# One decoder step in fp32 by split matmuls: which weight pieces are split ahead of time, and where the halves are kept

## The chip, the cores and the metric

The kernel runs on one core of a Trainium2 chip. The metric is the device time of one execution in microseconds (us); the time before is the median of three runs.

## The reference

A prompt of 256 tokens and 32 sample tokens (8 sequences of 4) go through two layers of width 2048. Each layer has a mixer and a dense squared-ReLU network, with an RMS norm ahead of and behind each. Cut to what the change touches:

```python
def _odd_mixer(h, conv_hist, w_in, ..., w_out):
    z = h @ w_in                                   # 2048 x 4096
    u, v, a, gate = jnp.split(z, [...])
    u = jax.nn.gelu(u)
    v = _ln(jax.nn.gelu(v), sg_ln_g, sg_ln_b)
    mixed = jnp.einsum('gij,bnjgc->bnigc', ws, vc) + sg_b   # causal gating within a chunk
    yc = u * mixed
    glu = a * jax.nn.sigmoid(gate)
    conv = depthwise_conv(concat([conv_hist, glu]), dw_w) + dw_b   # 31 taps, 1024 channels
    yd = jax.nn.silu(_ln(conv, cv_ln_g, cv_ln_b))
    return concat([yc, yd]) @ w_out

for l in range(2):                                 # l = 0: the even mixer (pooling, retention)
    h = h + _rms(mixer(_rms(h, ...)), ...)
    f = _rms(h, ...)
    f = jnp.square(jax.nn.relu(f @ w_up[l])) @ w_down[l]    # 2048 -> 8192 -> 2048
    h = h + _rms(f, ...)
```

## The kernel before

All 288 tokens stand as columns, features as partitions. A product of fp32 values is made of three fp32r matmuls: weights and activations are each split into a rounded part (`hi`) and the rest (`lo`), and hi·hi, lo·hi and hi·lo are summed in PSUM.

**Subs.** The weights come in 720 pieces, called subs, of 256 rows by 512 columns (512 KB). A sub is 24 matmuls (line 604): 2 row blocks, 4 column blocks `m`, 3 products. Eight subs (four in the odd layer's output projection) make a group, which fills four PSUM banks; the banks are read out behind its last sub (evictions). The subs in order: 0 to 79 input of the even mixer, 80 to 111 its output, 112 to 367 the first dense network (groups `w_up` and `w_down`, in four quarters), 368 to 431 input of the odd mixer, 432 to 463 its output in two halves, 464 to 719 the second dense network.

**How a sub is fed.** SP issues the load of `raw` (four buffers). ACT rounds it into `whi`, DVE subtracts into `wlo`: `A.activation(out=hi, in_=raws[p], func=AF.Copy)` in `emit_hi` and `V.tensor_tensor(out=lo, in0=raws.pop(p), in1=f(hi), op=SUB)` in `emit_lo`. `whi` and `wlo` have a ring of 3 slots, plus 1 (odd mixer) or 2 (dense networks) from a pool that is opened and closed by stage. A slot is free when TensorE has used its sub.

**Jobs and kept subs.** 60 subs of the odd mixer and of the second dense network's first group are split ahead. For each a job stands in the first dense network, behind its subs 1 and 5 of a group (`JOBS`): its raw load, ACT and DVE work are as a sub's, it takes a slot of the ring, and both halves are written to DRAM (`hik`, `lok`). Where the sub is due, SP loads both halves into its slot, with no work of ACT or DVE.

**Order of the work.** Each engine takes its instructions in the order in which `run` writes them. Around each sub, `run` writes the feeding of later subs, the sub's matmuls, evictions behind a last sub, and a step of each background generator (a `yield` ends a step). The odd mixer's background work is the convolution (`conv_all` on DVE with sums in PSUM, tile `cacc`; `conv_slow` on ACT and GpSimd; a load meter holds both back), the gating with its layer norm (`gating`), and behind the convolution `conv_out`: `layer_norm`, then Silu and splitting of 8 tiles. What is left of `conv_out` behind sub 447 is written at once (`bg_drain`), since sub 448 reads it.

**Norm boundaries.** The last group's squares are summed by one-column matmuls (`sum_part`), the last of them behind the last sub; then the scale is computed, spread and applied. `keep_warm` issues matmuls whose result nobody reads.

Of the kernel before, what the change touches and what calls it, by code (L numbers as in the profile page):

```python
# [178 lines left out]
def build(tc, ctx, I, O, C):  # L179
# [231 lines left out]
    def last_tiles(src, m):  # L411
# [61 lines left out]
    feed, pos, nraw, parts, kept = [], [], [], {}, {}  # L473
    RAW, RING = 4, 3
    JOBS = (1, 5)
# [16 lines left out]
    def emit_dma(p):  # L492
        kind, i = feed[p]
        if kind == "kept":
            return
# [16 lines left out]
    def emit_hi(p):  # L512
        kind, i = feed[p]
        hi, lo = parts[p] = ring_slot()
        if kind == "kept":
            for a, b in zip((hi, lo), kept[i]):
                SP.dma_start(out=f(a), in_=b)
        else:
            A.activation(out=hi, in_=raws[p], func=AF.Copy)
        if kind != "job":  # L520
            his[i] = hi, lo

    def emit_lo(p):
        kind, i = feed[p]
        hi, lo = parts.pop(p)
        if kind != "kept":
            V.tensor_tensor(out=lo, in0=raws.pop(p), in1=f(hi), op=SUB)
# [8 lines left out]
    def plan():  # L536

        todo = []
        where = {}
        at = 0  # L540
        for gi, g in enumerate(groups):
            for s in range(g.nsub):
                subs.append((g, s))
                if g.ahead and g.ahead(s):
                    todo.append(at + s)
            where[gi] = at
# [4 lines left out]
        ahead = set(todo)  # L551
        for i in range(len(subs)):
            pos.append(len(feed))
            feed.append(("kept" if i in ahead else "sub", i))
            if i in slots:
                feed.append(("job", slots[i]))
        n = 0
        for kind, i in feed:
            nraw.append(n)
            n += kind != "kept"  # L560
        nraw.append(n)

    def fetch():
        while W["dma"] < len(feed) and nraw[W["dma"]] < nraw[W["split"]] + RAW:
            emit_dma(W["dma"])
            W["dma"] += 1
# [14 lines left out]
    def some(n):  # L581

        return min(W["split"] + n - 1, pos[W["now"]] + RING + W["extra"] - 1)
# [66 lines left out]
    def run():  # L650
# [3 lines left out]
        for i, (g, s) in enumerate(subs):  # L654
# [29 lines left out]
            if last:  # L684
                if g.defer:
# [5 lines left out]
                    def rest(g=g):  # L691
                        yield from finish_pre(g.ready)
                        for m in range(0 if g.keep else 4):
# [36 lines left out]
    def ffn(layer, last):  # L730
        wu, wd = ("w_up", layer), ("w_down", layer)
        for q in range(4):
            for gm in range(4):
# [11 lines left out]
                def st_up(q=q, gm=gm):  # L745
                    if gm == 0:
# [4 lines left out]
                                  start=st_up, kouter=first, defer=first, jobs=() if last or first else JOBS,  # L751
                                  ahead=(lambda s: True) if last and first else None))
            for gm in range(4):
                def ev_dn(m, ps, gm=gm, q=q):
# [5 lines left out]
                    if q == 3:  # L760
# [3 lines left out]
                        else:  # L764
                            last_tiles(y(k), m)

                def fin_dn(q=q, gm=gm):
                    if q == 3 and gm == 3:
                        for m in range(4):
# [7 lines left out]
                                  jobs=() if last or (q == 3 and gm == 3) else JOBS))  # L777
# [331 lines left out]
    def even():  # L1109
# [35 lines left out]
        for gm in range(4):  # L1145
            def ev_o(m, ps, gm=gm):
# [5 lines left out]
                else:  # L1152
                    last_tiles(ps, m)
# [188 lines left out]
    def layer_norm(src, n, total, by_pe=False):  # L1342

        yield
        yield
# [25 lines left out]
        yield  # L1371
# [105 lines left out]
    def conv_out():  # L1477
# [4 lines left out]
        for k in range(8):  # L1482
# [6 lines left out]
            if k % 2 == 1:  # L1489
                yield  # L1490

    def odd():
# [9 lines left out]
        def ga(j):  # L1502
            def post_ga():
                if j == 1:
                    bg_drain(st_["setup"])
                if j == 0:
                    while "begun" not in Q:
# [9 lines left out]
                              ahead=lambda s: j == 0 or s % 2 == 1))  # L1517

        def vgrp(gm):
            def post_v():  # L1520
                if gm == 1:
# [5 lines left out]
                              post=post_v, ahead=lambda s: s % 2 == 1))  # L1527

        def ugrp(gm):
            def post_u():  # L1530
                if gm == 1:
                    bg_drain(st_["gate"])

                    def tail():
                        while any(c in bgs or c in fills for c in st_["conv"]):
# [7 lines left out]
                              start=start_u if gm == 0 else None, post=post_u, ahead=lambda s: s % 2 == 1))  # L1543
# [3 lines left out]
        for half in range(2):  # L1547
            for gm in range(4):
                def ev_o(m, ps, gm=gm, half=half):
# [5 lines left out]
                    else:  # L1555
# [4 lines left out]
                        else:  # L1560
                            last_tiles(y(k), m)

                def post_o(gm=gm, half=half):
                    if half == 0 and gm == 3:
                        for c in st_["conv"]:
# [13 lines left out]
                                  ahead=lambda s: s % 2 == 1))  # L1579
# [130 lines left out]
```

## Time and profile before

| | |
|---|---|
| runs | 2469.9, 2473.21, 2479.39 us; median 2473.21 |
| profiled execution | 2476.82 us, of it the span 2475.1 us |
| busy share of the span | TensorE 98%, DVE 55%, ACT 44%, GpSimd 10% |
| granted TensorE clock, mean | 0.988 |
| DMA | 529.35 MB, mean 214 GB/s |

How to read it: the span is the time from the first to the last instruction. TensorE's busy share counts pipelined matmuls and says little; what a stage loses is seen by its length against the number of its subs. Idle time of another engine costs something only where TensorE waits for it.

### The profile page before, as it was taken

To read this page: it belongs to the slowest core of one execution; us is meant where nothing else is said; L and a number is where in the kernel's file an instruction comes from. 1 tells how busy PE (TensorE), PEld (TensorE's weight loads), DVE (VectorE), ACT (ScalarE), POOL (GpSimd) and SP (SyncE) were. 2 spreads that over 40 slices of the span, in tenths; PEclk is the share of its full clock that TensorE was granted. 3 is DMA by queue.
4 is the path that set the end of the run, shared out by engine and by line. 5 is a ranking of instruction groups with operands and counts; after the bars stand their busy time and mean duration, and the time that the engine had idled before them with its cause. 6 is when DMAs were issued, how large, how long until landed. Compare 5 with 4: busy or idle time off the path is not lost.

```text
span 2475.1 us, 43388 instructions
## 1 busy us (share of the span) xinstructions
PE 2420.7 (98%) x17976; PEld 2386.2 (96%) x17976; DVE 1360.7 (55%) x1844; ACT 1090.6 (44%) x1567; POOL 251.9 (10%) x293
## 2 busy tenths in 40 slices
PE   9999999999999999999999999899999999999997
PEld 8899999999999999999999999899999999999997
DVE  5665564764455556555546976346434544544453
ACT  5343443554544455455434443435434434433442
POOL 0521111000000000000114750100000000000011
PEclk9999999999999999999999999999999999999998
DMA  7555464588888888888775656455555554545552
GB/s 253 164 185 181 159 206 160 181 280 296 289 289 297 279 295 290 294 288 293 261 254 211 246 200 219 179 196 190 168 164 168 163 169 161 172 162 170 165 166 92
DMA packets 146871, 529.35 MB, mean 214 GB/s; under 512 B 16809, under 2 KB 17849, under 8 KB 146649
## 3 DMA queue, kind: packets, MB, share of 16 engines
q1 hardware_dynamic: 142240, 511.81, 60.4%
q0 software_dynamic: 4288, 14.71, 1.8%
q8 instruction: 140, 2.29, 0.4%
q14 instruction: 59, 0.48, 0.1%
q10 hardware_dynamic: 144, 0.07, 0.0%
HBM read 453.68 MB, written 73.87 MB: 213 GB/s over the span
## 4 chain that ended last, share of the span: by engine, by line
PE 84%; DVE 6%; DMA 4%; ACT 3%; issue 2%; SPq 0%; POOL 0%; DVEq 0%; ACTq 0%; POOLq 0%
PE mm L604 81%; DVE wlo L162 2%; DVE cacc L162 2%; DMA raw<-in_wt 2%; DMA wlo<-lok 1%; ACT whi L162 1%; ACT tmp L162 1%; PE ms L313 1%; DMA lok<-wlo 1%; PE po L995 1%; DVE tmp L162 1%; PE ms L999 0%; DVE conv L162 0%; DVE yo L162 0%; PE ms L303 0%
## 5 line engine op out<-in xcount | busy, mean ns | idle before, releaser
L162 DVE TENSOR_TENSOR wlo<-raw,whi 128x1024 fp32r<-128x1024 f32 (+1 forms) x721 | 886.9, 1240 | 751.1 <-ACT whi L162 737.3
L162 ACT ACTIVATE whi<-raw 128x1024 fp32r<-128x1024 f32 (+1 forms) x721 | 755.1, 1057 | 1011.2 <-PE mm L604 892.1
L604 PE MATMUL mm<-xhi,wlo 128*128 128x288 f32 x3200 | 944.9, 297 | 11.3 <-DVE wlo L162 9.2
L604 PE MATMUL mm<-xhi,whi 128*128 128x288 f32 x3200 | 944.2, 297 | 10.3 <-DVE tmp L162 6.2
L604 PE MATMUL mm<-xlo,whi 128*128 128x288 f32 x3200 | 919.6, 296 | 0.0
L604 PE MATMUL mm<-hidhi,whi 128*128 128x288 f32 x2560 | 754.8, 296 | 6.8 <-ACT whi L162 3.2
L604 PE MATMUL mm<-hidhi,wlo 128*128 128x288 f32 x2560 | 757.6, 297 | 2.5 <-DMA wlo<-lok 1.7
L604 PE MATMUL mm<-hidlo,whi 128*128 128x288 f32 x2560 | 745.2, 296 | 0.0
L604 PEld LDWEIGHTS mm<-xhi,wlo 128*128 128x128 f32 x3200 | 605.4, 189 | 16.0 <-DVE wlo L162 13.2
L604 PEld LDWEIGHTS mm<-xhi,whi 128*128 128x128 f32 x3200 | 605.9, 189 | 13.3 <-issue 6.8
L604 PEld LDWEIGHTS mm<-xlo,whi 128*128 128x128 f32 x3200 | 595.8, 189 | 0.5 <-DVE xlo L162 0.5
L604 PEld LDWEIGHTS mm<-hidhi,whi 128*128 128x128 f32 x2560 | 485.3, 190 | 8.1 <-ACT whi L162 3.4
L604 PEld LDWEIGHTS mm<-hidhi,wlo 128*128 128x128 f32 x2560 | 485.4, 190 | 3.3 <-DMA wlo<-lok 2.1
L604 PEld LDWEIGHTS mm<-hidlo,whi 128*128 128x128 f32 x2560 | 480.3, 189 | 0.0
L162 POOL TENSOR_TENSOR acc<-acc,tmp 128x288 f32<-128x288 f32 x55 | 53.3, 970 | 1657.1 <-ACT tmp L162 1654.3
L162 DVE TENSOR_TENSOR y<-mm,y 128x288 f32<-128x288 f32 x112 | 50.9, 457 | 103.3 <-PE mm L604 103.3
L162 DVE SCALAR_TENSOR_TENSOR u<-mm,rb 128x288 f32<-128x288 f32 x120 | 54.3, 457 | 71.2 <-PE mm L604 71.2
L162 DVE SCALAR_TENSOR_TENSOR cacc<-gx,vecs,cacc 128x256 f32<-128x256 f32 x168 | 68.5, 478 | 0.0
L162 ACT ACTIVATE hidhi<-u 128x288 fp32r<-128x288 f32 x128 | 56.9, 445 | 4.1
L162 ACT ACTIVATE u<-u 128x288 f32<-128x288 f32 x128 | 55.3, 432 | 7.0 <-DVE u L162 6.9
L162 POOL TENSOR_TENSOR conv<-conv,tap 128x256 f32<-128x256 f32 x60 | 53.7, 895 | 13.6 <-ACT tap L162 10.0
L162 DVE TENSOR_TENSOR hidlo<-u,hidhi 128x288 fp32r<-128x288 f32 x128 | 49.7, 450 | 0.0
(180 smaller groups left out, 909.8 us busy)
## 6 DMA issues: line engine op xcount, KB each, us to landing
raw<-in_wt SPq DMA_DIRECT2D x719, 512.0 KB, 4.2
hik<-whi SPq DMA_DIRECT2D x60, 512.0 KB, 6.4
lok<-wlo SPq DMA_DIRECT2D x60, 512.0 KB, 7.1
whi<-hik SPq DMA_DIRECT2D x60, 512.0 KB, 4.4
wlo<-lok SPq DMA_DIRECT2D x60, 512.0 KB, 5.8
s0t<-in_state_ret POOLq DMA_DIRECT2D x24, 256.0 KB, 3.3
out<-s0t POOLq DMA_DIRECT2D x24, 256.0 KB, 3.4
out<-yo SPq DMA_DIRECT2D x8, 288.0 KB, 2.4
```

What stands on the lines that cost most here:

```text
L162: return call(*args, **kw)
L313: PE.matmul(P["sums"][:, t:t + 1], lhsT=a[:, c:c + 128], rhs=ones[:, 0:1], start=first and t == 0, stop=last and t == 2)
L604: PE.matmul(ps, lhsT=lhsT[:, k, c], rhs=rhs, start=s == 0 and k == 0 and which == 0, stop=s == g.nsub - 1 and k == 1 and which == 2)
L995: PE.matmul(po[gq:gq + 32, 0:256], lhsT=E["qdm"][:, hh, 32 * (b + i):32 * (b + i + 1)], rhs=s[:, i, :], start=False, stop=b >= 4, tile_pos ...
```

## The change

- **What is kept.** Only the `lo` half is written to DRAM and loaded back (`kept`); `hi` of such a sub is made again from `raw` where the sub is due, so its weights are loaded once more. DVE has nothing to do for it.
- **Where jobs put their halves.** Into buffers of their own (`jhi` once, `jlo` three times), no longer into slots of the ring.
- **Which subs.** All 64 of the odd mixer's input, and the 8 of the second dense network's first group. Those of the odd mixer's output are named too (every second sub of half 0, 8 in all), but the lambda reads `half` when `plan` runs, behind the loop, where it is 1: none of them is kept. So 72 jobs are made, not 80.
- **Where the jobs stand.** Behind subs 3, 5 and 7 of a group, from the third `w_up` group on.
- **Steps.** In `layer_norm` for the convolution two `yield`s go, and `conv_out` ends a step after four tiles, not two. `flush` (pending `hidlo` work) is called ahead of a deferred group's evictions.
- **A matmul.** `last_sums` issues `keep_warm(1)` ahead of the last sum, at three of the four boundaries.

```diff
-    JOBS = (1, 5)
+    JOBS = (3, 5, 7)
...
     def emit_hi(p):
         kind, i = feed[p]
-        hi, lo = parts[p] = ring_slot()
-        if kind == "kept":
-            for a, b in zip((hi, lo), kept[i]):
-                SP.dma_start(out=f(a), in_=b)
-        else:
-            A.activation(out=hi, in_=raws[p], func=AF.Copy)
-        if kind != "job":
-            his[i] = hi, lo
+        if kind == "job":
+            parts[p] = [W["pool"].tile([128, 2, 512], F32R, tag=t, name=t, bufs=n) for t, n in (("jhi", 1), ("jlo", 3))]
+            A.activation(out=parts[p][0], in_=raws[p], func=AF.Copy)
+            return
+        hi, lo = parts[p] = his[i] = ring_slot()
+        A.activation(out=hi, in_=raws[p], func=AF.Copy)
+        if kind == "lo":
+            SP.dma_start(out=f(lo), in_=kept[i])
...
         if kind == "job":
-            kept[i] = [dram.tile([128, 2, 512], F32, tag=f"{t}{i}", name=f"{t}k") for t in ("hi", "lo")]
-            W["out"] = [(b, a) for a, b in zip((hi, lo), kept[i])]
+            kept[i] = dram.tile([128, 2, 512], F32, tag=f"k{i}", name="kept")
+            W["out"] = [(kept[i], lo)]
...
-        return min(W["split"] + n - 1, pos[W["now"]] + RING + W["extra"] - 1)
+        return min(W["split"] + n - 1, pos[min(W["now"] + RING + W["extra"], len(subs)) - 1])
...
-                                  start=st_up, kouter=first, defer=first, jobs=() if last or first else JOBS,
-                                  ahead=(lambda s: True) if last and first else None))
+                                  start=st_up, kouter=first, defer=first, jobs=() if last or (q == 0 and gm < 2) else JOBS,
+                                  ahead=(lambda s: "lo") if last and first else None))
...
         elif i == 1:
             sum_part(P.pop(("own", 2)))
+            if P.pop("rest"):
+                keep_warm(1)
             sum_part(P.pop(("own", 3)), last=True)
...
     def layer_norm(src, n, total, by_pe=False):
 
         yield
-        yield
+        if not by_pe:
+            yield
...
-                              ahead=lambda s: j == 0 or s % 2 == 1))
+                              ahead=lambda s: "lo"))
...
-                                  ahead=lambda s: s % 2 == 1))
+                                  ahead=lambda s: "lo" if half == 0 and s % 2 else None))
```

Three places show how instructions move. First DVE in the odd mixer's input, up to the eviction (`tmp<-mm,rb`) behind sub 399; `cacc` and `conv` are the convolution. Before:

```order
L162 SCALAR_TENSOR_TENSOR cacc<-gx,vecs,cacc 128x256 x4
L162 TENSOR_TENSOR wlo<-raw,whi 128x1024
L162 TENSOR_REDUCE conv<-prod 128x32
L162 TENSOR_SCALAR conv<-conv,vecs 128x32
L162 SCALAR_TENSOR_TENSOR cacc<-gx,vecs,cacc 128x256 x8
L162 TENSOR_TENSOR wlo<-raw,whi 128x1024
L162 SCALAR_TENSOR_TENSOR cacc<-gx,vecs,cacc 128x256 x15
L162 TENSOR_TENSOR tmp<-mm,rb 128x288 x4
```

And in the changed kernel, up to the same eviction:

```order
L162 TENSOR_REDUCE conv<-prod 128x32
L162 TENSOR_SCALAR conv<-conv,vecs 128x32
L162 SCALAR_TENSOR_TENSOR cacc<-gx,vecs,cacc 128x256 x6
L162 SCALAR_TENSOR_TENSOR conv<-gx,vecs,cacc 128x256
L162 SCALAR_TENSOR_TENSOR cacc<-gx,vecs,cacc 128x256
L162 TENSOR_TENSOR conv<-cacc,conv 128x256
L162 TENSOR_SCALAR cacc<-gx,vecs 128x256 x2
L162 SCALAR_TENSOR_TENSOR cacc<-gx,vecs,cacc 128x256 x18
L162 TENSOR_TENSOR tmp<-mm,rb 128x288 x4
```

The `wlo` rows are gone, and convolution work stands in their place. Second, DVE at the convolution's layer norm (`conv<-conv,mean`) and behind it (`tmp<-conv,rl`, `hidlo`). Before, where sub 448's `wlo` is the last one ahead of `tmp<-conv,rl`, and three more pairs of the last two rows follow with no `wlo` between them:

```order
L162 TENSOR_TENSOR conv<-cacc,conv 128x256
L162 TENSOR_TENSOR wlo<-raw,whi 128x1024 x2
L162 TENSOR_TENSOR conv<-conv,mean 128x288 x8
L162 TENSOR_TENSOR wlo<-raw,whi 128x1024
L162 TENSOR_SCALAR sm_86<-ms 128x3
L162 TENSOR_TENSOR wlo<-raw,whi 128x1024
L162 TENSOR_TENSOR tmp<-conv,rl 128x288 x2
L162 TENSOR_TENSOR hidlo_16946<-tmp,hidhi_16945 128x288 x2
```

In the changed kernel, beginning at the eviction behind sub 431; the four `wlo` in one row are those of subs 437 to 440:

```order
L162 TENSOR_TENSOR tmp<-mm,rb 128x288 x4
L162 TENSOR_TENSOR wlo<-raw,whi 128x1024
L162 TENSOR_TENSOR tmp<-mb,ug 128x288 x4
L162 TENSOR_TENSOR hidlo_16332<-tmp,hidhi_16331 128x288 x4
L162 TENSOR_TENSOR conv<-conv,mean 128x288 x4
L162 TENSOR_TENSOR wlo<-raw,whi 128x1024
L162 TENSOR_TENSOR conv<-conv,mean 128x288 x4
L162 TENSOR_TENSOR wlo<-raw,whi 128x1024
L162 TENSOR_SCALAR sm_86<-ms 128x3
L162 TENSOR_TENSOR wlo<-raw,whi 128x1024 x4
L162 TENSOR_TENSOR tmp<-conv,rl 128x288 x4
```

The layer norm stands eight subs earlier, and the tiles behind it are done near sub 441, not behind sub 447. On TensorE its one-column sums move from ahead of subs 442 and 443 to ahead of subs 434 and 435. Third, SP in the odd mixer's input, with what each issue waits for (`DMAHW` is an earlier transfer). Before:

```order
L503 DMA raw<-in_wt 128x1024 [waits DMAHW3_49,DVE_49]
L517 DMA whi<-hik 128x1024 [waits DMAHW5_49,DMAHW4_49,PE_49]
L517 DMA wlo<-lok 128x1024 [waits DMAHW6_49]
L503 DMA raw<-in_wt 128x1024 [waits DVE_49]
L517 DMA whi<-hik 128x1024 [waits DMAHW7_49,DMAHW1_49,PE_49]
```

And in the changed kernel:

```order
L522 DMA wlo<-kept 128x1024 [waits DMAHW7_49,PE_49]
L504 DMA raw<-in_wt 128x1024 [waits DMAHW0_49,Activation_49]
L522 DMA wlo<-kept 128x1024 [waits DMAHW1_49,PE_49]
L504 DMA raw<-in_wt 128x1024 [waits DMAHW2_49,Activation_49]
L522 DMA wlo<-kept 128x1024 [waits DMAHW3_49,PE_49]
```

A raw load here waits for ACT, no longer for DVE, and two loads a sub follow each other through all 64 subs.

## Rows read from the trace of the kernel before

**Rows 1.** Windows, weight matmuls (line 604) alone: busy us of PE, PEld; PEclk; DMA.

```profile
405.20:437.10 31.90, 25.78 (x194) 25.33 (x192) 1.00 0.42 133
437.10:548.80 111.70, 106.44 (x769) 103.70 (x770) 0.98 0.68 233
548.80:1234.20 685.40, 685.40 (x5186) 685.40 (x5186) 1.00 0.84 289
1234.20:1268.30 34.10, 26.06 (x195) 25.41 (x193) 0.95 0.70 230
1268.30:1327.20 58.90, 54.23 (x385) 52.83 (x386) 0.97 0.69 257
1327.20:1505.60 178.40, 159.84 (x1153) 156.91 (x1153) 0.97 0.60 215
1505.60:1569.90 64.30, 57.30 (x385) 55.84 (x385) 0.92 0.53 189
1569.90:1592.60 22.70, 16.91 (x97) 16.02 (x97) 0.85 0.52 193
1592.60:1640.10 47.50, 38.51 (x291) 38.09 (x289) 0.93 0.71 262
1640.10:1744.30 104.20, 102.62 (x769) 101.91 (x770) 1.00 0.50 167
```

**Rows 2.** Waits of PE from 1327.2 to 1505.7 us: sum, times, longest.

```profile
PE mm L604 <- DVE tmp L162: 8.3, 4, 3.0
PE ms L1439 <- DVE mb L162: 2.9, 1, 2.9
```

**Rows 3.** Waits of PE from 1268.3 to 1327.2 us.

```profile
PE mm L604 <- DMA wlo<-lok: 2.0, 2, 1.2
PE mm L604 <- DMA whi<-hik: 1.3, 1, 1.3
```

**Rows 4.** Waits of PE from 1569.9 to 1592.6 us.

```profile
PE mm L604 <- ACT whi L162: 3.2, 1, 3.2
...
PE mm L604 <- DVE wlo L162: 0.9, 1, 0.9
```

**Rows 5.** Windows, all engines: PE, PEld, DVE, ACT, POOL; PEclk; DMA share, GB/s.

```profile
1327.20:1505.60 178.40, 167.19 (x1233) 165.18 (x1233) 149.79 (x291) 76.21 (x140) 109.84 (x117) 0.97 0.60 215
1356.47:1359.88 3.41, 3.41 (x16) 3.41 (x15) 3.31 (x7) 0.00 (x0) 1.74 (x4) 0.50 0.00 0
```

**Rows 6.** Groups of DVE by form, 1327.2 to 1505.6 us.

```profile
L162 DVE SCALAR_TENSOR_TENSOR cacc<-gx,vecs,cacc 128x256 f32<-128x256 f32 x153 | 62.3, 478 | 0.0
L162 DVE TENSOR_TENSOR wlo<-raw,whi 128x1024 fp32r<-128x1024 f32 x24 | 38.0, 1582 | 13.1 <-ACT whi L162 13.1
```

**Rows 7.** Timeline of DVE ahead of the group end at 1355 us.

```profile
1340.03 1.23 DVE L162 TENSOR_TENSOR wlo<-raw,whi 128x1024 fp32r<-128x1024 f32 x1 [4.20 <-ACT whi L162]
1346.15 3.12 DVE L162 TENSOR_TENSOR wlo<-raw,whi 128x1024 fp32r<-128x1024 f32 x1
1349.19 5.96 DVE L162 SCALAR_TENSOR_TENSOR cacc<-gx,vecs,cacc 128x256 f32<-128x256 f32 x15
```

**Rows 8.** Timeline of POOL at the same place.

```profile
1345.09 3.10 POOL L162 TENSOR_TENSOR prod<-gx,vecs 128x992 f32<-128x992 f32 x1
```

**Rows 9.** Timeline of PE: three unread matmuls at a boundary; wait ahead of the last sum.

```profile
435.34 1.70 PE L369 MATMUL ms<-acc,cg 128*128 128x288 f32 x6
...
1633.27 1.44 PE L313 MATMUL ms<-cg,tmp 128*128 128x1 f32 x6 [0.52 <-ACT tmp L162]
```

**Rows 10.** Windows, all engines, columns as in rows 5: two stretches of dense loads.

```profile
5.00:15.00 10.00, 7.81 (x50) 6.64 (x49) 7.26 (x13) 7.53 (x13) 0.00 (x0) 1.00 1.01 399
1264.00:1296.00 32.00, 30.85 (x211) 29.23 (x210) 20.33 (x43) 10.76 (x23) 3.10 (x5) 0.95 0.86 313
```

**Rows 11.** Page, DMA issues: count, KB each, median us to landing.

```profile
wlo<-lok SPq DMA_DIRECT2D x60, 512.0 KB, 5.8
```

**Rows 12.** Chain of waits: start us, us, what.

```profile
1264.01 12.57 DMA wlo<-lok
```

More of the change, by code (lines that the diff above doesn't have):

```diff
@@ L409, in scale_y, with last_tiles @@
         A.activation(out=y(k), in_=y(k), func=AF.Copy, scale=gain(which, layer, k))
-    def last_tiles(src, m):
+    def last_tiles(src, m, rest):
+        P["rest"] = rest
         if m < OWN:
@@ L472, in build @@
     subs = []
-    feed, pos, nraw, parts, kept = [], [], [], {}, {}
+    feed, pos, parts, kept = [], [], {}, {}
     RAW, RING = 4, 3
-    JOBS = (1, 5)
+    JOBS = (3, 5, 7)
     raws, his = {}, {}
@@ L493, in emit_dma @@
         kind, i = feed[p]
-        if kind == "kept":
-            return
         g, s = subs[i]
@@ L525, in emit_lo @@
         hi, lo = parts.pop(p)
-        if kind != "kept":
-            V.tensor_tensor(out=lo, in0=raws.pop(p), in1=f(hi), op=SUB)
+        raw = raws.pop(p)
+        if kind != "lo":
+            V.tensor_tensor(out=lo, in0=raw, in1=f(hi), op=SUB)
         if kind == "job":
-            kept[i] = [dram.tile([128, 2, 512], F32, tag=f"{t}{i}", name=f"{t}k") for t in ("hi", "lo")]
-            W["out"] = [(b, a) for a, b in zip((hi, lo), kept[i])]
+            kept[i] = dram.tile([128, 2, 512], F32, tag=f"k{i}", name="kept")
+            W["out"] = [(kept[i], lo)]
     def put_out():
@@ L536, in plan @@
     def plan():
-        todo = []
+        todo, kinds = [], {}
         where = {}
@@ L543, in plan @@
                 subs.append((g, s))
-                if g.ahead and g.ahead(s):
+                kind = g.ahead(s) if g.ahead else None
+                if kind:
                     todo.append(at + s)
+                    kinds[at + s] = kind
             where[gi] = at
@@ L550, in plan @@
         slots = dict(zip(slots, todo))
-        ahead = set(todo)
         for i in range(len(subs)):
             pos.append(len(feed))
-            feed.append(("kept" if i in ahead else "sub", i))
+            feed.append((kinds.get(i, "sub"), i))
             if i in slots:
                 feed.append(("job", slots[i]))
[L557 to L561, printed above, removed]
     def fetch():
-        while W["dma"] < len(feed) and nraw[W["dma"]] < nraw[W["split"]] + RAW:
+        while W["dma"] < len(feed) and W["dma"] < W["split"] + RAW:
             emit_dma(W["dma"])
@@ L692, in rest @@
                         yield from finish_pre(g.ready)
+                        flush()
                         for m in range(0 if g.keep else 4):
@@ L764, in ev_dn @@
                         else:
-                            last_tiles(y(k), m)
+                            last_tiles(y(k), m, True)
                 def fin_dn(q=q, gm=gm):
@@ L776, in ffn @@
                                   post=to_odd if q == 3 and gm == 1 and not last else None,
-                                  jobs=() if last or (q == 3 and gm == 3) else JOBS))
+                                  jobs=() if last or (q == 3 and gm > 0) else JOBS))
     evo, ne = _cols(C_EVEN)
@@ L1370, in layer_norm @@
         yield
-        yield
+        if not by_pe:
+            yield
         pb = spread(rs)
@@ L1488, in conv_out @@
             late(lambda hl=hl, s=s, hh=hh: V.tensor_tensor(out=hl, in0=s, in1=f(hh), op=SUB))
-            if k % 2 == 1:
+            if k % 4 == 3:
                 yield
@@ L1526, in vgrp @@
                               lambda m, ps: ev_v_odd(m, ps, gm), start=start_v_odd if gm == 0 else None,
-                              post=post_v, ahead=lambda s: s % 2 == 1))
+                              post=post_v, ahead=lambda s: "lo"))
         def ugrp(gm):
@@ L1542, in ugrp @@
             groups.append(Grp(w, [(512 * gm, 512)], list(range(KT)), xs, lambda m, ps: ev_u(m, ps, gm),
-                              start=start_u if gm == 0 else None, post=post_u, ahead=lambda s: s % 2 == 1))
+                              start=start_u if gm == 0 else None, post=post_u, ahead=lambda s: "lo"))
         for fn, i in ((ga, 0), (ga, 1), (ga, 2), (vgrp, 0), (vgrp, 1), (ga, 3), (ugrp, 0), (ugrp, 1)):
@@ L1560, in ev_o @@
                         else:
-                            last_tiles(y(k), m)
+                            last_tiles(y(k), m, True)
                 def post_o(gm=gm, half=half):
```

3 lines of the change are left out of this document (1 added, 2 removed).

## The prediction

> **What bounds the kernel now.** I read the stages first, by windows that hold the weight matmuls alone [rows 1]. From 548.8 to 1234.2 us, 216 subs take 685.4 us, so a sub that waits for nothing takes 3.173 us; the granted clock there is 1.00. 720 subs at this pace would be 2285 us. What a stage loses is its length less its subs times 3.173:
>
> - 405.2 to 437.1, 8 subs (25.4): 6.5, a norm boundary at full clock
> - 437.1 to 548.8, 32 subs (101.5): 10.2, the start of the first dense network
> - 1234.2 to 1268.3, 8 subs: 8.7, the next boundary
> - 1268.3 to 1327.2, 16 subs (50.8): 8.1, the odd mixer's first two input groups
> - 1327.2 to 1505.6, 48 subs (152.3): 26.1, the rest of its input
> - 1505.6 to 1569.9, 16 subs: 13.5, output half 0, with the convolution's layer norm
> - 1569.9 to 1592.6, 4 subs (12.7): 10.0, the first group of half 1
> - 1592.6 to 1640.1, 12 subs (38.1): 9.4, with a boundary
> - 1640.1 to 1744.3, 32 subs: 2.7, the start of the second dense network
>
> Then the waits of TensorE: in the rest of the odd mixer's input four times the evicting `tmp` of DVE, 8.3 us in all, and once DVE's `mb`, 2.9 [rows 2]; in its first two groups loads of kept halves, 2.0 and 1.3 [rows 3]; in half 1 `whi` and `wlo` of a sub behind the drained tail, 3.2 and 0.9 [rows 4]. Behind such a wait the clock stands at its lower level for a while, 0.50 from 1356.47 to 1359.88 [rows 5], with 16 matmuls where the pace has 26. A window's clock loss is its length times one less the granted clock: 0.03 of 178.4, 5.4 us, from 1327.2; 0.15 of 22.7, 3.4 us, from 1569.9 [rows 1].
>
> Why DVE is late at those group ends: from 1327.2 to 1505.6 it is busy for 149.8 us [rows 5] of the 152.3 that the stage should last, 38.0 of it for 24 `wlo`, and stands idle 13.1 more because a `wlo` at the head of its queue waits for ACT's `whi` [rows 6]. Just ahead of the end at 1355 us, a 4.20 us idle time and a `wlo` of 3.12 us in place of 1.23 are followed by 15 `cacc` in 5.96, and the eviction stands behind these [rows 7].
>
> That long `wlo` lies beside GpSimd's `prod` of 3.10 us [rows 8], while `cacc`, with one operand in PSUM, keeps its 0.40 beside GpSimd's work. The Trainium skill (GPSIMD Engine Reference, Specifications) says that GpSimd's way into SBUF is shared with VectorE and contended by VectorE instructions with two inputs in SBUF. The trace agrees. By that rule the 24 removed `wlo` free their contended 38.0 us; at the uncontended 1.23 they would free 29.5.
>
> **The change part by part.** All terms are against the profiled execution, 2476.82 us (the span and 1.7 around it), which lies 3.6 above the median 2473.21.
>
> 1. *DVE in the odd mixer's input.* No `wlo` is left there: 38.0 us of work and the 13.1 of idle time go. The order shows more convolution in their place, but only what came later before: 168 less 153, 15 `cacc` at 0.40, 6 us. DVE's load falls to about 118 of 152.3 us. The waits for it are 8.3 and 2.9, and the clock behind them 5.4: 16.6. I take 13, since bursts stay (up to 18 `cacc` and two more in one run ahead of an eviction, 8 us where 15 took 6, and GpSimd is still beside it). Ends: 18 (with the clock behind the last wait, counted in the next window), and 6 slower, if each of the first three ends comes 2 us later. The other 9.5 of the stage are mostly TensorE's own work for gating, which stays.
>
> 2. *Feeding of subs 368 to 383.* Waits for kept halves there are 3.3, and the clock 0.03 of 58.9, 1.8. SP's raw loads stood behind DVE's sums of squares; now they wait for ACT. ACT has 12 more `whi` there at about 1.05, which fit between its other work but can be late for a sub by a microsecond. I take 4; ends 5 and minus 3.
>
> 3. *The convolution's tail.* Before, 8 tiles of `tmp`, Silu and splits were written in one piece behind sub 447, and three `whi` and `wlo` behind them: TensorE waits 3.2 for `whi`, then for `wlo` and loads, at 0.85 of its clock. In the changed order this work stands between the `wlo` of 440 and 442. Of the 10.0 I take 9.5; ends 10 and 7 (the waits for ACT and DVE and the clock: 3.2, 0.9, 3.4).
>
> 4. *The layer norm itself* moves eight subs up. Its one-column sums are the same work; a short wait for a kept load goes; but it now meets the end of the gating, with 8 splits of `tmp<-mb,ug` ahead of it on DVE. 0; ends plus and minus 3.
>
> 5. *The unread matmul.* Three of them take 1.70 [rows 9], 0.57 each, and the place ahead of the last sum has an idle time of 0.52 that ACT's square ends. So it is nearly hidden: if not, 1.7 for three. What it may give is the clock: boundaries at lower clock lose 8.7 and 9.4 where one at full clock loses 6.5, so at most 2.2 and 2.9. I take 2, nearer the middle, because one wait less at the first (an eviction behind a job) belongs to it as well. Ends 5 and minus 1.7.
>
> 6. *Jobs in the first dense network.* The first two groups have none now, and jobs leave the ring alone. The same start without jobs, in layer 1, loses 2.7 where this one loses 10.2: at most 7.5. Layer 1's first subs are split ahead and layer 0's aren't (about 2), so I take 5; ends 7.5 and 0. In the steady stretch a group moves 8 loads and 3 times 1.05 MB, 7.3 MB, as before (8 loads and 2 times 1.57), so its 289 GB/s stays; ACT and DVE have 12 jobs more, hidden beside matmuls that lose nothing there now.
>
> 7. *What is added.* Eight `whi` between the `xhi` at sub 464, and 16 subs of the output made in place rather than loaded, on engines that are idle half the time there: 0.5; ends 0 and 3 slower.
>
> Sum: 13 + 4 + 9.5 + 0 + 2 + 5 − 0.5 = 33. 2476.8 − 33 = 2443.8 for an execution like the profiled one, and 2440 against the median. All upper ends together are 49 (2424), all lower ends about 10 slower (2483).
>
> **Rivals.**
>
> *A: the convolution takes the room.* The meter lets convolution in whenever DVE's load falls, so the backlog ahead of an eviction stays. For it: the order's 18 `cacc`. Against it: the 13.1 us of idle time behind `whi` cannot return. Part 1 gives nothing: gain 20, 2453.
>
> *B: transfers become the bound.* Each of 64 subs now loads 1.05 MB in 3.173 us, 330 GB/s; the longest stretch with loads that dense ran at 313 (share 0.86), the steady one at 289 (0.84); but ten microseconds ran at 399 [rows 1, 10]. At 289 a sub takes 3.63: 0.455 for the 56 subs that had less before, 25 us. Gain 8, 2465. The Trainium skill (DMA: Bandwidth & Descriptors, Bandwidth) has 341 GB/s for a transfer of 1 MB and less for smaller ones. By that figure a sub's two loads take an estimated 3.07 us, just inside the pace, and smaller ones would miss it; the row of 399 speaks against taking this as a ceiling.
>
> *C: slower, because a kept half lands late.* Its load is issued when a ring slot comes free, three subs ahead, 9.5 us; it lands after a median of 5.8 [rows 11], but 12.57 was seen once, in a burst [rows 12]. If loads behind each other on SP's queue take that long in the whole input, a sub lasts a third of it, 4.19: 57 us over 56 subs, and 33 less 57 is 24 slower, 2497. It decides from about 11.3 us a landing (three times 3.173 + 33/56).
>
> *D: the steady stretch pays for its jobs.* Three a group, two subs apart, come closer together than two; if 60 of them cost TensorE 0.3 us each, 18 us, 2458. Against it: DVE is not on TensorE's path there with two a group.
>
> **How the numbers follow.** Forecast 0.67, A 0.15, B 0.08, C 0.05, D 0.05. The predicted time is 2440. The forecast's own spread is about 12 either way; reaching up over A and D gives 2424 to 2461, with B, C and a part of the tails outside. Half a per cent of 2473, 12.4 us, is about what a measurement of this kernel can tell from no change: faster (below 2461) 0.86, same 0.09 (B, a part of D), slower 0.05 (C).
>
> **What would show it.** Right: no `wlo` and no idle time behind `whi` on DVE from 1300 to 1480 us, the clock at 1.00 over its group ends; four subs behind the half at about their 12.7 us; the stretch from 437 us about 5 shorter; the steady stretch still 3.173 a sub. Wrong: waits for `wlo<-kept` in the odd mixer's input with a DMA share near 1 (B) or landings above 9.5 us (C); waits for `tmp` as before (A); any loss from 549 to 1234 us (D).

## The result, and the profile after

The changed kernel takes 2447.97 us (median of 4 runs, 2445.86 to 2452.39) where the kernel before, beside it, takes 2473.42: ratio 0.9897, 95% interval 0.9873 to 0.9921, 25.4 us less. Predicted were 2440, a range of 2424 to 2461, and faster with a chance of 0.86. The profiled execution took 2445.86, its span 2444.2, which is 30.9 less than the span before.

Windows that hold the weight matmuls alone (now line 601), at the same subs as [rows 1] from its second row on; columns as there:

```profile
438.50:546.00 107.50, 104.32 (x768) 102.04 (x769) 1.00 0.61 207
546.00:1231.40 685.40, 685.40 (x5186) 685.40 (x5185) 1.00 0.78 268
1231.40:1263.90 32.50, 25.85 (x194) 25.40 (x192) 1.00 0.62 208
1263.90:1320.50 56.60, 53.11 (x385) 51.27 (x386) 1.00 0.84 326
1320.50:1482.80 162.30, 154.82 (x1153) 152.65 (x1153) 1.00 0.86 302
1482.80:1551.10 68.30, 54.70 (x386) 53.44 (x385) 0.93 0.37 120
1551.10:1563.80 12.70, 12.70 (x98) 12.70 (x97) 1.00 0.73 249
1563.80:1609.00 45.20, 38.54 (x291) 38.09 (x289) 1.00 0.54 187
1609.00:1713.60 104.60, 103.02 (x768) 101.90 (x769) 1.00 0.53 182
```

Each stage's length less its subs times 3.173 is what it loses. In the order of the program, before and after (from the matmuls' own starts, to 0.1):

| subs | stage | before | after | gained | foreseen |
|---|---|---|---|---|---|
| 0–79 | even mixer's input | 66.9 | 68.2 | −1.2 | nothing |
| 112–143 | start of the first dense network | 10.1 | 6.0 | 4.1 | 5 (term 6) |
| 144–359 | its steady stretch | 0.1 | 0.1 | 0 | 0 |
| 360–367, 460–463 | two boundaries | 18.1 | 14.1 | 4.0 | 2 (term 5) |
| 368–383 | odd mixer's first two groups | 8.1 | 5.8 | 2.3 | 4 (term 2) |
| 384–431 | rest of its input | 26.2 | 10.1 | 16.1 | 13 (term 1) |
| 432–447 | output half 0, layer norm | 13.5 | 17.5 | −4.0 | 0 (term 4) |
| 448–451 | first group of half 1 | 10.0 | 0.0 | 10.0 | 9.5 (term 3) |
| 464–495 | start of the second dense network | 2.6 | 3.1 | −0.5 | −0.5 (term 7) |

The sum is 30.8 of the 30.9 between the spans. Every window whose clock was below 1.00 before is at 1.00 now and shorter, but for one: the window from 1482.8 stands at 0.93 and is longer. Each row is read from one profile of either kernel. In the second profile of the changed kernel (run 10) 432–447 lose 19.1, so the −4.0 would be −5.6 there; the other rows from 112 on differ by 0.5 or less between the two.

TensorE's waits from 1320.5 to 1482.9 us, which answer to [rows 2]; the 8.3 us for `tmp` are gone:

```profile
PE ms L1439 <- DVE mb L162: 0.5, 1, 0.5
```

From 1263.9 to 1320.6 us, as [rows 3]:

```profile
PE mm L601 <- DMA wlo<-kept: 1.8, 3, 1.4
PE mm L601 <- ACT whi L162: 0.2, 1, 0.2
```

All engines from 1320.5 us, columns as in [rows 5], and two of DVE's groups there, as [rows 6]. Of the 24 `wlo` two are left. They belong to the next stage's first subs and stand at the end, at 1475.3 and 1479.5, with 1.1 us of idle time behind `whi` in place of 13.1:

```profile
1320.50:1482.80 162.30, 161.77 (x1233) 160.56 (x1233) 127.95 (x286) 99.44 (x164) 93.59 (x118) 1.00 0.86 302
```

```profile
L162 DVE SCALAR_TENSOR_TENSOR cacc<-gx,vecs,cacc 128x256 f32<-128x256 f32 x168 | 67.8, 480 | 0.0
L162 DVE TENSOR_TENSOR wlo<-raw,whi 128x1024 fp32r<-128x1024 f32 x2 | 2.4, 1223 | 1.1 <-ACT whi L162 1.1
```

And the new wait, of TensorE from 1482.8 to 1551.2 us; the 3.2 and 0.9 of [rows 4] have no counterpart behind it:

```profile
PE mm L601 <- ACT y L162: 8.2, 1, 8.2
```

The timeline of ACT ahead of it shows why. Sub 439's last matmul starts at 1514.93, and sub 440 needs the banks that `y<-mm` reads out. ACT first waits 3.14 for DVE, then does four tiles of Silu and `hidhi` (the first is shown) and a `whi`, and only then the eviction:

```profile
1513.88 1.04 ACT L162 ACTIVATE whi<-raw 128x1024 fp32r<-128x1024 f32 x1
1518.06 0.63 ACT L162 ACTIVATE tmp<-tmp,vecs 128x288 f32<-128x288 f32 x1 [3.14 <-DVE tmp L162]
1518.72 0.44 ACT L162 ACTIVATE hidhi<-tmp 128x288 fp32r<-128x288 f32 x1
...
1522.05 1.04 ACT L162 ACTIVATE whi<-raw 128x1024 fp32r<-128x1024 f32 x1
1522.99 1.28 ACT L162 COPY y<-mm 128x288 f32<-128x288 f32 x4
```

DVE is late because of ACT: the second piece's `tmp<-conv,rl` stand behind a `wlo` that waits 2.96 for ACT's `whi`, which ACT has only behind the first piece, and behind four `hidlo`:

```profile
1514.96 1.23 DVE L162 TENSOR_TENSOR wlo<-raw,whi 128x1024 fp32r<-128x1024 f32 x1 [2.96 <-ACT whi L162]
1516.10 1.56 DVE L162 TENSOR_TENSOR hidlo<-tmp,hidhi 128x288 fp32r<-128x288 f32 x4
1517.57 1.19 DVE L162 TENSOR_TENSOR tmp<-conv,rl 128x288 f32<-128x288 f32 x3
```

Behind the wait the clock is at its lower level, 1.2 GHz (all engines):

```profile
1518.13:1528.37 10.24, 4.95 (x20) 4.95 (x21) 5.19 (x9) 6.97 (x14) 0.00 (x0) 0.50 0.31 96
```

### The profile page after: what moved, and what is told of

It is laid out like the page before. It is cut to its first block, busy times and chain, and to the rows that moved or that the text cites. A ratio compares the mean times of both kernels' runs of the same rounds, so it can differ in the third digit from the quotient of the medians.

```text
span 2444.2 us, 43553 instructions
## 1 busy us (share of the span) xinstructions
PE 2404.5 (98%) x17982; PEld 2371.2 (97%) x17982; DVE 1360.8 (56%) x1844; ACT 1163.2 (48%) x1639; POOL 238.1 (10%) x293
## 4 chain that ended last, share of the span: by engine, by line
PE 92%; DVE 3%; ACT 2%; issue 1%; DMA 1%; POOL 0%; SPq 0%; DVEq 0%; ACTq 0%; POOLq 0%
PE mm L601 89%; DVE wlo L162 1%; ACT whi L162 1%; ACT tmp L162 1%; DMA raw<-in_wt 1%; PE ms L313 1%; PE po L993 1%; PE ms L997 0%; DMA wlo<-kept 0%; PE ms L303 0%; DVE yo L162 0%; DVE y L162 0%; DVE h L162 0%; DVE xlo L162 0%; DVE hidlo L162 0%
## 5 line engine op out<-in xcount | busy, mean ns | idle before, releaser
L162 DVE TENSOR_TENSOR wlo<-raw,whi 128x1024 fp32r<-128x1024 f32 (+1 forms) x649 | 795.2, 1230 | 630.5 <-ACT whi L162 629.3
L601 PEld LDWEIGHTS mm<-xhi,wlo 128*128 128x128 f32 x3200 | 602.1, 188 | 14.1 <-DVE wlo L162 11.2
L162 DVE TENSOR_TENSOR jlo<-raw,jhi 128x1024 fp32r<-128x1024 f32 x72 | 88.1, 1223 | 62.8 <-ACT jhi L162 55.0
L162 ACT ACTIVATE jhi<-raw 128x1024 fp32r<-128x1024 f32 x72 | 75.9, 1055 | 56.0 <-DMA raw<-in_wt 54.2
L162 ACT ACTIVATE u<-u 128x288 f32<-128x288 f32 x128 | 55.3, 432 | 10.5 <-DVE u L162 10.2
```

What stands on the lines that cost most here:

```text
L162: return call(*args, **kw)
L601: PE.matmul(ps, lhsT=lhsT[:, k, c], rhs=rhs, start=s == 0 and k == 0 and which == 0, stop=s == g.nsub - 1 and k == 1 and which == 2)
```

## The experiments

Losses are worked out as in the table, from one profile each; ratios are to the kernel before, run on the same chip. One `yield` more moves the background work that follows it behind the next sub.

**1. The layer norm's two steps put back.**

```diff
         yield
-        if not by_pe:
-            yield
+        yield
         ps = bank()
...
-        if not by_pe:
-            yield
+        yield
         pb = spread(rs)
```

> The changed kernel with the two steps of the convolution's layer norm put back (four-tile steps of Silu and splits stay). Theory: the changed kernel's wait of 8.2 us at sub 440, for the eviction y<-mm of subs 436 to 439, is there because the second four-tile step stands ahead of that eviction on ACT, and the clock behind it is at its lower level for 10.24 us, worth about 5.1; with two more steps both pieces stand behind the eviction, so the stretch of subs 432 to 447 loses about 6 us instead of 17.4, and the time is about 25 + 11 = 36 us below the kernel before (about 2437). The tail behind sub 447 stays free, since the freed DVE, not the fewer steps, lets the convolution end early. Rival: the fewer steps are what brings the pieces ahead of sub 448; putting the steps back costs the 9.5 us of the tail again, about 16 us below the kernel before (about 2457).

Measured: 2452.47, ratio 0.9913 (0.99 to 0.9926). The tail of half 1 stayed free (448 to 451 lose 0.0), so the fewer steps aren't what freed it. But 432 to 447 lost 20.6, not 6: the pieces now stand behind the eviction of 436 to 439 and ahead of that of 440 to 443, which TensorE waits for instead, and its one-column sums wait as well:

```profile
PE mm L601 <- ACT y L162: 4.6, 1, 4.6
PE ms L313 <- ACT tmp L162: 1.3, 2, 0.8
```

Each theory had one half: the wait was rightly named, but it moved instead of going.

**2. The two-tile steps put back as well.**

```diff
-            if k % 4 == 3:
+            if k % 2 == 1:
                 yield
```

> The changed kernel with the layer norm's two steps and the two-tile steps put back, so that of the change the kept halves, their buffers and places and the unread matmul are left. Theory: as with the layer norm's steps alone put back: no 8.2 us wait at sub 440, no stretch at the lower clock, tail behind sub 447 free; about 2437, 36 us below the kernel before, within 3 us of the other. Rival: two-tile steps spread to subs 442 to 445 run into the end of half 0, and the first four subs of half 1 lose some 5 us: about 2442. Second rival, the prediction's own: without the fewer steps the tail costs 9.5 again, about 2457.

Measured: 2455.43, ratio 0.9926 (0.9914 to 0.9939), and 432 to 447 lost 24.8. The wait for the same eviction is longer:

```profile
PE mm L601 <- ACT y L162: 8.9, 1, 8.9
```

ACT's timeline shows what a step costs: three times it waits 2.40 for DVE ahead of a piece, and a piece of two tiles and its `whi` comes every 5.46:

```profile
1530.22 0.63 ACT L162 ACTIVATE tmp<-tmp,vecs 128x288 f32<-128x288 f32 x1 [2.40 <-DVE tmp L162]
...
1535.68 0.63 ACT L162 ACTIVATE tmp<-tmp,vecs 128x288 f32<-128x288 f32 x1 [2.40 <-DVE tmp L162]
```

From 432 to 451 this kernel loses 24.8, the kernel before 23.5, the changed one 17.5. So the earlier end of the convolution, by itself, moves the drained work to another eviction and gains nothing there. The 7.3 between run 2 and the changed kernel are not mainly the eviction's: the two subs at the late eviction lose 10.7 in the changed kernel, 7.3 in run 1 and 11.5 in run 2. The three subs at the one-column sums lose 5.6, 12.1 and 12.0, and there the clock is at its lower level for 10.2 us in runs 1 and 2, and not at all in the changed kernel's profile. The same sums with the changed steps lose between 7.1 and 10.2 in runs 4, 5 and 7 to 11, so a part of the 7.3 is this profile's and not the steps'. My theory for both runs fell; the rivals' time (2457) was nearer, by a way that they did not name.

**3. The new steps alone, in the kernel before.** (The lines of runs 1 and 2, the other way round.)

> The kernel before with the changed steps alone (two steps of the layer norm less, four-tile steps). Theory: the layer norm still starts near sub 441, since DVE is as full as before; all eight tiles of Silu and splits then stand between the eviction of subs 440 to 443 and that of subs 444 to 447, and TensorE waits for that last eviction instead of for whi and wlo behind it: the stretch of subs 432 to 451 loses 20 to 27 us where it lost 23.5, the time is within 4 us of the kernel before (2469 to 2477). Rival, the prediction's term 3 as a matter of the steps: the 9.5 us of the tail go, about 2464.

Measured: 2467.99, ratio 0.9979 (0.9969 to 0.999): 5.7 us less than before, between the two. In the profile 432 to 447 lose 9.1 and 448 to 451 lose 5.3, 9.2 less in all. So the steps alone take half of the tail behind sub 447; with DVE freed it went whole, without them too (runs 1 and 2).

**4. No unread matmul.**

```diff
-            if P.pop("rest"):
-                keep_warm(1)
+            P.pop("rest")
```

> The changed kernel without the unread matmuls ahead of the last sums. Theory: they hold the clock at the two odd boundaries (subs 360 to 367 and 460 to 463), which lost 8.7 and 9.4 us before and lose 7.0 and 7.0 in the changed kernel; without them both show a lower clock again, the two boundaries lose 4 us more, and the time is about 21 us below the kernel before (about 2452). Rival: the clock there is lost for what happened ahead of the boundary (waits for evictions and jobs in the last group), which the other parts of the change removed; then both boundaries stay at 1.00 and the time is that of the changed kernel, about 2448, or 2447 if the matmuls cost 0.5 each.

Measured: 2451.75, ratio 0.9911 (0.9899 to 0.9924). Both boundaries have a lower mean clock again and lose 8.2 and 8.3 where the changed kernel loses 7.1 each:

```profile
1232.85:1266.46 33.61, 25.80 (x195) 25.38 (x193) 0.95 0.65 209
1593.62:1614.57 20.95, 13.10 (x98) 12.68 (x97) 0.92 0.55 201
```

With the matmul (the first row; each unread matmul leaves two records) the last sum, which waited 0.52 for ACT [rows 9] and waits 0.52 again in this run, starts without a wait:

```profile
1603.85 0.73 PE L369 MATMUL ms<-acc,cg 128*128 128x288 f32 x2
1604.52 0.83 PE L313 MATMUL ms<-cg,tmp 128*128 128x1 f32 x6
```

Over all profiles of this study, with other edits among them, one of these two boundaries fell to the lower clock in 1 of 22 places with the matmul and in 5 of 6 without it. The sixth, subs 460 to 463 of run 3, kept the clock without the matmul and lost 7.1, as with it: so the matmul itself costs nothing there. So the matmul does hold the clock, for 1.2 us a boundary rather than the 2 of the theory. This stands on the profiles: by the time, the interval overlaps that of the changed kernel, and that it met the theory's 2452 is chance in part, since 432 to 447, which the edit doesn't touch, lose 20.3 in this profile, 2.8 more. The other 1.7 of the 4.0 in the table are not the matmul's, as the two lost 18.1 in the kernel before and 16.5 here: 0.5 is a wait for `y` at the first boundary, gone in this run, and the rest, at the second, goes with a longer stretch at the lower clock (6.8 us for 3.4).

**5. One more step between the two pieces.**

```diff
             if k % 4 == 3:
                 yield
+            if k == 3:
+                yield
```

> The changed kernel with one more step between the first four and the last four tiles of Silu and splits, so that the eviction of subs 436 to 439 stands between the two pieces on ACT. Theory: the wait of 8.2 us at sub 440 comes from the second piece alone, which stands ahead of that eviction; the first piece is over when sub 439 ends. The stretch of subs 432 to 447 loses about 7 us (5.5 of it the one-column sums on TensorE) instead of 17.5; time about 2438, 35 us below the kernel before. Rival: ACT and DVE wait for each other in each piece, so the late work only moves on to the next eviction, as it did with the layer norm's steps put back (4.75 and 2.53 at subs 443 and 444); then the stretch loses 14 or more and the time is 2445 to 2450.

Measured: 2441.5, ratio 0.9874 (0.986 to 0.9888). The eviction now stands between the pieces, and the wait falls from 8.2 to

```profile
PE mm L601 <- ACT y L162: 1.0, 1, 1.0
```

Subs 439 and 440 lose 9.4 less, nearly the 10.5 of the theory. Yet the stretch loses 12.7, not 7: at the one-column sums the clock is at its lower level for 10.2 us in this profile, and subs 433 to 435 lose 10.2 in place of 5.6. In time it is 6.7 below run 8, which ran beside it without the step (and with eight more subs kept). So the place of the wait is shown, and the rival, by which it moves on, falls: no other eviction is waited for.

**6. Every second sub kept.**

```diff
-    ahead=lambda s: "lo"))
+    ahead=lambda s: "lo" if j == 0 or s % 2 else None))
...
-    post=post_v, ahead=lambda s: "lo"))
+    post=post_v, ahead=lambda s: "lo" if s % 2 else None))
```

(and the same behind `post_u`).

> The changed kernel, in which only every second sub of the odd mixer's input behind its first group is kept (36 of 64, as many as the kernel before kept there; the lo half alone, buffers and steps as changed). Theory: what the stage of subs 384 to 431 gained (26.2 us of loss down to 10.1) is DVE's, by the wlo that no longer stand on its queue; with 28 of them back the stage loses 20 to 26 again, the convolution ends late, and the tail costs up to 10 more: 2458 to 2472. Rival: it came from jobs that leave the ring alone or from raw loads that no longer wait for DVE, which stay here; then the stage loses 10 to 14 and the time is 2448 to 2453.

Measured: 2467.44, ratio 0.9983 (0.9973 to 0.9993). Subs 384 to 431 lose 28.1, more than the 26.2 of before, and the waits and DVE's `wlo` of [rows 2, 6] are back:

```profile
PE mm L601 <- DVE tmp L162: 6.2, 3, 3.0
PE ms L1439 <- DVE mb L162: 3.4, 1, 3.4
```

```profile
L162 DVE TENSOR_TENSOR wlo<-raw,whi 128x1024 fp32r<-128x1024 f32 x25 | 41.2, 1647 | 10.1 <-ACT whi L162 9.9
```

This settles term 1: the `wlo` on DVE's queue are what the stage lost, by the evictions behind them. The jobs' buffers were as in the changed kernel. The raw loads of these subs wait for DVE's `wlo` again (SP: 101.7 us in 22 waits), which no run tells apart from the `wlo`; but TensorE has no wait for `whi`, `wlo` or a load in the stage, so it is not by late feeding that they cost.

**7. Both halves kept.**

```diff
-    (("jhi", 1), ("jlo", 3))
+    (("jhi", 2), ("jlo", 2))
...
-        A.activation(out=hi, in_=raws[p], func=AF.Copy)
-        if kind == "lo":
-            SP.dma_start(out=f(lo), in_=kept[i])
+        if kind == "lo":
+            for a, b in zip((hi, lo), kept[i]):
+                SP.dma_start(out=f(a), in_=b)
+        else:
+            A.activation(out=hi, in_=raws[p], func=AF.Copy)
```

(with no raw load of such a sub, and both halves written by its job).

> The changed kernel, but both halves of each of the 72 kept subs are written and loaded back, as in the kernel before; buffers of the jobs two and two. A sub loads as many bytes as with lo and raw (1.05 MB), a job writes twice as much. Theory: the gain is DVE's, and which half ACT makes again doesn't matter: subs 384 to 431 lose 10 as in the changed kernel, the time is within 4 us of 2448. Rival 1: loading hi is late, since its load can start only when the slot of the ring is free, while raw has buffers of its own: waits for whi<-hik, as in the first two input groups of the kernel before (1.3 and 2.0), come at many subs, 368 to 431 lose 10 to 30 us more, 2458 to 2478. Rival 2: the double writes fill the queues of the steady stretch (8 loads and three times 1.57 MB a group, 8.9 MB in 25.4 us, 351 GB/s), and subs 144 to 359, which lose 0.07 now, lose 10 or more.

Measured: 2457.06, ratio 0.994 (0.9928 to 0.9952). Subs 384 to 431 lose 9.7, as with `lo` alone, so there the theory holds and rival 1 falls. The 9 us are lost where the jobs are made: 112 to 143 lose 11.1 instead of 6.0, and the steady stretch 5.9 instead of 0.1, with five waits for DVE's evictions. The first row is the whole of that stretch, the second the part with jobs in it, at 347 GB/s; the changed kernel's part with jobs (546 to 1093 us) ran at 291 with a share of 0.84 and lost nothing:

```profile
549.61:1240.85 691.24, 687.06 (x5187) 685.66 (x5186) 1.00 0.87 316
549.61:1098.00 548.39, 544.24 (x4108) 543.07 (x4107) 1.00 0.95 347
```

```profile
PE mm L609 <- DVE u L162: 2.3, 2, 1.3
PE mm L609 <- DVE y L162: 1.8, 3, 1.0
```

Rival 2 is right about the place and the rate (351), with half its price. In the stretch ACT waits 250.8 us for raw loads, 143.9 in the changed kernel, which speaks for the fuller queues; but the buffers (two and two) were changed with the writes, and the two were not told apart. Keeping `lo` alone pays in the making, not in the use.

**8. Output half 0 kept as well.**

```diff
-    ahead=lambda s: "lo" if half == 0 and s % 2 else None))
+    ahead=lambda s, half=half: "lo" if half == 0 and s % 2 else None))
```

> The changed kernel with the value of half bound where the group is made, so that the eight subs of output half 0 are kept as well (80 jobs). Theory: DVE's wlo of every second sub of 432 to 447 goes, so DVE is earlier at the tiles of Silu, and the wait of 8.2 us at sub 440 shrinks by 1 to 3 us; the 8 more jobs cost nothing in the steady stretch: 2445 to 2447. Rival: the wait is ACT's own queue (four tiles of 1.06 us and a whi ahead of the eviction), and nothing changes: 2448. Second rival: kept halves land late while the layer norm runs (TensorE waits for wlo<-kept), 2449 to 2453.

Measured: 2448.16, ratio 0.9902 (0.989 to 0.9915), no change. The wait at sub 440 shrank by 3.4 (4.8 in place of 8.2), but this profile's clock fell at two boundaries, and its boundary at 1233 us lost 9.5, the one place of the 22. The time is the first rival's, 2448; the wait is the theory's. So this run decides nothing on what the eight subs are worth.

**9. Jobs from the second group on.**

```diff
-    jobs=() if last or (q == 0 and gm < 2) else JOBS,
+    jobs=() if last or first else JOBS,
```

> The changed kernel with jobs from the first dense network's second group on, as in the kernel before (behind subs 3, 5 and 7 there; the last three of the job places at the end stay empty). Theory (the prediction's term 6): what subs 112 to 143 gained (10.1 us of loss down to 6.0) is that no job stands in the second group while the boundary's work runs; with them back the waits for wlo at sub 122 (0.9) and for u at sub 136 (2.2, with the clock behind it) return, and the stretch loses 9 to 10: about 2452. Rival: it is the jobs' own buffers that gained it, since a job took a slot of the ring before; then the stretch loses 6 to 7 as in the changed kernel, 2448.

Measured: 2455.14, ratio 0.9932 (0.9919 to 0.9944), against 2448.17 for the changed kernel beside it. The stretch loses 9.8: the size was right. The wait is another one (the two for `wlo` in the second line stand in the changed kernel too). GpSimd's `sm` of the boundary's second sum waits for DVE's, and that stands behind a `wlo` that waited for ACT, in a group with a job's `jlo` in it:

```profile
PE ms L303 <- POOL sm L162: 3.4, 1, 3.4
PE mm L601 <- DVE wlo L162: 1.2, 2, 0.7
```

```profile
492.06 1.23 DVE L162 TENSOR_TENSOR wlo<-raw,whi 128x1024 fp32r<-128x1024 f32 x1 [1.28 <-ACT whi L162]
493.20 0.15 DVE L162 TENSOR_SCALAR sm<-ms 128x3 f32<-128x3 f32 x1
```

**10. The changed kernel again.** Not an edit, a measure of the others.

> The changed kernel once more, beside the others of this call: 2448, 25 us below the kernel before (its first time: 2447.97, ratio 0.9897); the profiled stages as before within 3 us in all, but for the first two subs, which have lost 3.0 to 6.1 us in the profiles so far.

Measured: 2448.17, ratio 0.9902 (0.9888 to 0.9915). Its profile's span is 3.4 longer than the first one's, half of it in 432 to 447 (19.1 for 17.5, with another 3.4 us at the lower clock). So much is the noise of a loss that is read from one profile.

**11. Runs 5 and 8 together.**

> The changed kernel with one more step between the two pieces of Silu and splits, and the eight subs of output half 0 kept as well. Theory: the step left 1.0 us of the wait at sub 440, and the kept subs alone took 3.4 off it; together no wait is left there, 1 to 2 us below the step alone (2441.5, ratio 0.9874). Rival: the eight more loads meet the layer norm's stretch and take back what they give, 2441 to 2443.

Measured: 2441.61, ratio 0.9876 (0.9861 to 0.9891). A wait of 0.8 for `y` is left of 1.0: no gain on run 5. The time is the rival's; its reason is not shown, as TensorE waits for no load in 432 to 447.

**12. Run 5, and the squares added in pairs.**

```diff
-                sum_part(sq, k == 0, k == 7)
+                if k % 2:
+                    V.tensor_tensor(out=sq, in0=sq, in1=even, op=ADD)
+                    sum_part(sq, k == 1, k == 7)
+                even = sq
```

> The changed kernel with one more step between the two pieces, and with the squares of the convolution's layer norm added in pairs on DVE ahead of their one-column sums (12 of these matmuls in place of 24, and four additions on DVE). Theory: subs 433 and 434 lose the sums' own 5.5 us of TensorE, at about 0.24 each with what lies between, and the clock falls for them; half of them saves 2.8 and some of the clock, 2437 to 2439. Rival: DVE's additions wait for ACT's squares and TensorE for the additions, so the sums end as late as now and a wait stands in their place: 2441 to 2443.

Measured: 2439.38, ratio 0.9865 (0.9852 to 0.9879), the lowest of all: about 9 us below the changed kernel. Its interval overlaps that of run 5, so of its two edits only the first is shown by the time. In the profile 432 to 447 lose 8.6 instead of 12.7, but most of that goes with the clock (3.4 us at its lower level for 10.2): subs 433 to 435 lose 6.0 where run 5 lost 10.2, and the changed kernel, with all 24 sums and its clock up, lost 5.6 there. So what the pairs are worth is not shown. The rival's wait is there too, but small:

```profile
PE ms L313 <- DVE tmp L162: 1.3, 2, 0.7
PE mm L601 <- ACT y L162: 1.0, 1, 1.0
```

## Why the prediction was right, and where it was off

The signs named for being right came: the clock at 1.00 over the group ends, 12.7 us for the four subs behind the half, a start of the first dense network shorter by 4.1, and 3.173 a sub in the steady stretch.

*Term 1 (13, measured 16.1)* is shown by run 6. The 16.6 of waits and clock went but for a wait of 0.5, since no eviction was late at all: the bursts that I kept 3 us for did not hold one up. DVE was busy for 128 us of the stage rather than 118.

*Term 2 (4, measured 2.3).* Waits for kept halves stayed, 1.8 for 3.3; the clock's part came. No run tried this term by itself, and other profiles with these 16 subs kept as changed lose 4.8 to 7.0, so its size is known to a microsecond only.

*Terms 3 and 4 (9.5 and 0, measured 10.0 and −4.0)* belong together. That the tail behind sub 447 goes was right. The step that failed is term 4: I counted the layer norm's own work and what stood ahead of it on DVE, with ends of 3 either way, and did not ask what is queued behind the moved tiles on ACT. It is an eviction, and it costs 8.2 and the clock behind it: the two subs there lose 10.7. Runs 1 and 2 showed that the place of these steps decides which eviction waits, run 5 that a step between the pieces takes the wait away.

*Term 5 (2, measured 4.0)* is in its ends; run 4 puts 2.3 of it on the matmul, and one wait less (0.5) was foreseen as well.

*Term 6 (5, measured 4.1)* is shown by run 9 in place and size, not in mechanism: the waits of before that I named for run 9 were not the ones that came back.

*Term 7 (−0.5)* came as foreseen, within what profiles differ by (run 10 loses 0.3 more there), and in the steady stretch nothing was lost. That stretch didn't stay at 289 GB/s, as term 6 had it, but moved 268: the last job is written out at 1096 us, and behind it the rate is 173.

*The rivals.* A did not come: 15 more `cacc` moved in, and TensorE waited for no `tmp`. Nor did B: the stage ran at 302 GB/s with a share of 0.86 and no wait for a load. Where transfers may begin to bind is seen in run 7, whose steady stretch lost 5.9 with 347 GB/s and a share of 0.95 while it had jobs. The Trainium skill (DMA: Bandwidth & Descriptors, Bandwidth) has 341 GB/s for a transfer of 1 MB; run 7's 347 over 548 us of 512 KB transfers, loads and writes together, lies a little above it, so here that figure is no ceiling. C did not come: a kept half landed after a median of 5.0 us where [rows 11] have 5.8 (from the page's DMA issues):

```profile
wlo<-kept SPq DMA_DIRECT2D x72, 512.0 KB, 5.0
```

D came only in run 7, a third of its price.

*From 33 to 25.* In the profiles the terms gave 32.0 of the 33, and 0–79, which no term names, lost 1.2. That the sum came so near is luck in part: terms 1, 3 and 5 gave 5.6 more than foreseen, terms 2, 4 and 6 gave 6.6 less. The other 5.5, from 30.9 to 25.4, lie between executions: the profiled one of before was 3.4 above its median, that of the changed kernel 2.1 below its own. I took the gain against an execution on the slow side of its kernel and subtracted it from the median, which was already without a part of it.

Not tried apart are the other lines of the change: the new bound in `some`, `flush` ahead of a deferred group's evictions, the jobs' places behind subs 3, 5 and 7 of a group, and their own buffers by themselves.

## What to carry to other kernels

When an engine that feeds and evicts is full, take whole operations off its queue; here 22 fewer of 1.6 us were worth 16. When steps of background work move, look on every engine for the eviction that now stands behind them: work that ends sooner can still stand in front of something due earlier. Work split ahead has a price in two places, where it is made and where it is used. Look at both: with both halves kept (run 7) the use lost nothing more, and the making lost 11 us.

## What was not expected of the hardware

GpSimd's same 60 additions of the convolution took 895 ns each before and 750 in the changed kernel, with DVE's `wlo` gone (from 1327.2 us before, from 1320.5 after):

```profile
L162 POOL TENSOR_TENSOR conv<-conv,tap 128x256 f32<-128x256 f32 x60 | 53.7, 895 | 13.6 <-ACT tap L162 10.0
```

```profile
L162 POOL TENSOR_TENSOR conv<-conv,tap 128x256 f32<-128x256 f32 x60 | 45.0, 750 | 34.6 <-ACT tap L162 31.1
```

With every second `wlo` back (run 6) they took 909, and the `wlo` 1647, where the two left in the changed kernel took 1223. So `wlo` and GpSimd's work, beside each other, slow each other, as the long `wlo` of [rows 7] let one suspect. The Trainium skill (GPSIMD Engine Reference, Specifications) has GpSimd's way into SBUF as shared with VectorE, with contention by instructions with two inputs in SBUF, as `wlo` is one. These rows agree with it, on GpSimd's side.

In 8 of 14 profiles the clock was at its lower level for a while near 13 us, in the others not; subs 0 to 79, the same instructions in all, lose 68.2 to 70.2 there and 66.5 to 67.3 otherwise. The changed kernel (first row) and the kernel before, in the same stretch, all engines:

```profile
12.85:16.27 3.42, 3.42 (x17) 3.42 (x16) 3.07 (x4) 1.38 (x3) 0.00 (x0) 0.50 1.03 420
```

```profile
12.85:16.27 3.42, 3.42 (x28) 3.42 (x27) 3.26 (x5) 1.57 (x3) 0.00 (x0) 1.00 1.02 420
```

What decides it was not found; it makes about 2 us of the difference between profiles.
